# Turning the decayed keys on VectorE where they are made, in a decoder trunk on one core

## The chip, the core and the metric

The kernel runs on one core of a Trainium2 chip. A core has TensorE (PE: matmuls; a matmul first loads a stationary operand, "PEld", then streams a moving one, and writes to PSUM), VectorE (DVE), ScalarE (ACT), GpSimd (POOL) and SyncE (SP), which issues nearly all DMA here. Each engine works through its own list of instructions in order; semaphores hold an instruction until what it needs is there. DMA moves data between the device's memory (DRAM in the kernel's words) and the on-chip memory SBUF. The metric is the device time of one execution in microseconds, as the median of several runs.

## The reference

One layer of a decoder trunk over 1024 tokens of width 1024, all in float32. Two branches share one input projection: gated linear attention (GLA, 4 heads, keys of 128, values of 256) and a gated short convolution. They are merged, projected, and followed by a gated embedding and a norm. What matters here is the attention, in chunks of 64 tokens:

```python
b = jnp.cumsum(gk, axis=3)
b_last = b[:, :, :, -1:, :]
q_in = q * jnp.exp(b)
k_in = k * jnp.exp(-b)
k_dec = k * jnp.exp(b_last - b)
a = jnp.where(causal, jnp.einsum('nbhid,nbhjd->nbhij', q_in, k_in), 0.0)
o_intra = jnp.einsum('nbhij,nbhjv->nbhiv', a, v)

def step(state, xs):
    q_n, k_n, v_n, d_n = xs
    o_n = jnp.einsum('bhcd,bhdv->bhcv', q_n, state)
    state = d_n[..., None] * state + jnp.einsum('bhcd,bhcv->bhdv', k_n, v_n)
    return state, o_n
```

The state's update multiplies the decayed keys `k_dec`, turned, with the values. On TensorE the contraction runs over the partitions, so the update needs `k_dec` with tokens on the partitions, while the input projection makes it with the key's 128 features on the partitions.

## The kernel before

**Matmuls.** Nearly all work on TensorE is products of 1024-wide matrices. They are cut in quadrants by Strassen's scheme in Winograd's form (seven products for eight, classes `Cell` and `Rows`), and every float32 operand is split into a high and a low part (`split`: ScalarE copies the high part, VectorE subtracts it), so that a product is three matmuls (`mm3`). A product of one quadrant is 12 matmuls of 128x128 by 512 columns. `run_groups` runs the products in a fixed order; it asks for a product's loads up to 14 products ahead (`RING` = 8 plus 6) and for its splits up to 7 ahead.

**Order of the work.** Nothing is issued as the code runs. `Flow.note` records each instruction with a modelled cost, and finds what it depends on by blocks of `GRAIN` elements along a tile's free dimension (`View.blocks`, L122 to 130). `set_dues` gives every instruction a due time and `put_in_order` simulates the five engines and writes one order for each. The large products' matmuls (`main`) keep the program's order; the attention's matmuls come in bundles (`nc.bundle`, `close_bundle`) that are put between them when their operands are ready by the simulation.

**Where the keys are made.** In the phase "qk", `k_cons` (L1343 to 1360) takes a head's k for one half of the tokens (512) from PSUM, with the 128 features on the partitions. It fills the tile `kk`: for each of NP = 4 pairs of chunks (128 tokens) 4 x 64 columns, of which the first 128 are the scores' keys and the last 128 the decayed keys as the state needs them. One store puts both in `qkd[h][i]`, columns 384 to 640 of a row of 5 x 128 per pair. `q_cons` puts the scaled q into the first three blocks. There are 4 heads and 2 halves, so this happens 8 times.

**Where they are used.** `attend` (L1445 to 1563) goes over 8 pairs of chunks for 2 heads, twice (32 steps in all). `fetch` loads a step's 5 x 128 columns (`qkl`) and the values (`vl`) three steps ahead. `step_a` computes the scores (the float32 matmul is recorded as two instructions) and turns the decayed keys with a TensorE transpose into columns 128 to 256 of the PSUM tile `X`, except in a head's last pair, whose state nobody reads. `read_a` takes the scores through the mask and splits them (`aTh`, `aTl`), and splits the turned keys from PSUM into `keh` and `kel`. In the next bundle `step_s` multiplies these with the values for the state's update and `step_b` computes the output; `read_s` and `read_b` take them out of PSUM.

**The gate's input.** Late in the kernel `flip` turns the residual in blocks and stores it in `gd[p][j][:, i]`, from where the gate's cells load it.

`ev` (L892) is a pool of three 128x512 tiles, shared by several phases.

Of the kernel before, what the change touches and what calls it, by code (L numbers as in the profile page):

```python
# [16 lines left out]
P = 128  # L17
# [6 lines left out]
NP = HALF // P  # L24
# [18 lines left out]


PE, DVE, ACT, POOL, SP = range(5)
GRAIN = 64
TABLE = {AF.Exp: 1, AF.Ln: 2, AF.Sigmoid: 3}


class View:  # L50
# [81 lines left out]
    def place(self):  # L132
        real = self.buf.get()
        if self.dtype != self.buf.dtype:
            real = real.bitcast(self.dtype)
        a, b = self.rows
        return bass.AP(tensor=real.tensor, offset=real.offset + a * self.buf.size + self.off,
                       ap=[[self.buf.size, b - a]] + [[s, n] for s, n in self.dims])


class Buffer:
# [105 lines left out]
class Flow:  # L247
# [12 lines left out]
    def note(self, engine, op, call, args, kw):  # L260
        views = [a for a in args if isinstance(a, View) or hasattr(a, "ap")]
        views += [a for k, a in kw.items() if k not in ("out", "accum_out") and (isinstance(a, View) or hasattr(a, "ap"))]
        outs, ins = ([kw["out"]], views) if "out" in kw else (views[:1], views[1:])
        if kw.get("accum_out") is not None:
            outs.append(kw["accum_out"])
        o = Op()
        o.n, o.engine, o.call, o.args, o.kw = len(self.ops), engine, call, args, kw
        o.side, o.table, o.bytes, o.bufs, o.hurry = self.side, 0, 0, [], self.hurry
        label = lambda v: v.buf.name if isinstance(v, View) else "in"
        o.name = f"{label(outs[0])}<-{','.join(label(v) for v in ins)}"  # L270
        shape = outs[0].shape
        n = 1
        for d in shape[1:]:
            n *= d
        o.lat = 0.15
        if op == "dma_start":
            o.cost, o.bytes = 0.4, shape[0] * n * 4
            o.lat = 2.0 + o.bytes / 250e3
        elif engine == PE:
            o.cost, o.lat = n / 2400 + 0.0134, 0.22  # L280
            if op == "transpose" or args[1].dtype == F32:
                o.cost = 0.11 if op == "transpose" else 0.22
            elif args[1].shape[0] < P:
                o.cost = 0.42
        elif engine == DVE:
            psum = any(isinstance(v, View) and v.buf.pool.name == "ps" for v in outs + ins)
            o.cost = 0.07 + n * (0.00055 if op in ("tensor_scalar", "tensor_copy") and not psum else 0.00104)
            if op in ("scalar_tensor_tensor", "tensor_scalar"):
                o.cost += 0.06
            if op == "tensor_tensor_scan":  # L290
                o.cost = 0.05 + n * 0.0021
        elif engine == ACT:
            o.cost = 0.10 + n * 0.000833 + (0.1 if "accum_out" in kw else 0.0) + (0.08 if len(ins) > 1 else 0.0)
            o.table = TABLE.get(args[2] if len(args) > 2 else None, 0)
        elif engine == POOL:
            o.cost = 0.1 + n * 0.001 if op == "memset" else 0.35 + 0.25 * n
        preds = {}

        def behind(p):
            if p is not None and p != o.n:  # L300
                q = self.ops[p]
                lat = q.lat
                if q.engine == engine and not q.bytes:
                    lat = 0.0 if engine == PE else 0.08
                preds[p] = max(preds.get(p, 0.0), lat)

        for v in ins:
            if isinstance(v, View):
                for b in v.blocks():
                    e = v.buf.memory.setdefault(b, [None, []])  # L310
                    behind(e[0])
                    e[1].append(o.n)
        for v in outs:
            if isinstance(v, View):
                for b in v.blocks():
                    e = v.buf.memory.setdefault(b, [None, []])
                    for p in [e[0]] + e[1]:
                        behind(p)
                    e[0], e[1] = o.n, []
                if engine == PE:  # L320
                    behind(v.buf.group)
                    v.buf.group = o.n
                for pool in v.buf.pool.instead:
                    for old in pool.buffers:
                        for p in old.users:
                            behind(p)
        for v in outs + ins:
            if isinstance(v, View) and v.buf not in o.bufs:
                if v.buf.index is None:
                    v.buf.index = len(v.buf.tag.buffers)  # L330
                    v.buf.tag.buffers.append(v.buf)
                o.bufs.append(v.buf)
                v.buf.users.append(o.n)
        o.preds, o.succs = preds, []
        for p in preds:
            self.ops[p].succs.append(o.n)
        self.ops.append(o)
        if engine == PE and not o.side:
            self.main.append(o)
        if self.bundle is not None and engine == PE:  # L340
            self.bundle.append(o)
# [195 lines left out]
def kernel(  # L537
# [56 lines left out]
    def dram(name, *shape):  # L594
        return dr.tile([P, *shape], F32, name=name)
# [11 lines left out]
    mcd = [[dram(f"mcd{k}_{i}", HALF) for i in range(2)] for k in range(8)]  # L607
    md = [dram(f"md{i}", 2, 2, 2, 4, P) for i in range(2)]
    x2d = [dram(f"x2d{b}", D) for b in range(8)]
    gd = [[dram(f"gd{p}_{q}", 2, 4, P) for q in range(2)] for p in range(4)]  # L610
    wtd = [[dram(f"wtd{w}_{n}", 4, 512) for n in range(4 + 3 * w)] for w in range(2)]

    load = nc.sync.dma_start
# [693 lines left out]
    with phase("qk", [ph["za"]]) as qp:  # L1307
# [35 lines left out]
        def k_cons(hp):  # L1343

            def cons(i, j, src):
                h = 2 * hp + j
                nm = f"{h}_{i}"
                c4 = get_c(h, i, "k")
                kk = qp.tile([P, NP, 4, CH], F32, tag="kk", name=f"kk{nm}", bufs=2)
                dc = dcs[:, h, i]  # L1350
                tt(kk[:, :, 0:4:3, :], c4, c4[:, :, :, CH - 1:CH].to_broadcast([P, NP, 2, CH]), op=ALU.subtract)
                ex(kk[:, :, 0:4:3, :], kk[:, :, 0:4:3, :], 1.0)
                ex(kk[:, :, 1, :], c4[:, :, 1, :], 1.0)
                k4 = src.rearrange("p (n c t) -> p n c t", c=2, t=CH)
                tt(kk[:, :, 0, :], k4[:, :, 0, :], kk[:, :, 0, :], op=ALU.mult)
                tt(kk[:, :, 1:4:2, :], k4[:, :, 1:2, :].to_broadcast([P, NP, 2, CH]), kk[:, :, 1:4:2, :],
                   op=ALU.mult)
                tt(kk[:, :, 2, :], kk[:, :, 0, :], dc[:, :, 1:2].to_broadcast([P, NP, CH]), op=ALU.mult)
                store(qkd[h][i][:, :, 3 * P:5 * P], kk.rearrange("p n s t -> p n (s t)"))
            return cons  # L1360

        for hp in range(2):
# [82 lines left out]
    def attend(hp, ap, every):  # L1445
# [21 lines left out]
        def step_a(it, X):  # L1467
            pr, h = its[it]
            qk = f(ins[it][0])
            mm(X[:, 0:P], qk[:, 3 * P:4 * P], qk[:, 2 * P:3 * P], start=True, stop=True)  # L1470
            if pr < 2 * NP - 1:
                transpose(X[:, P:2 * P], qk[:, 4 * P:5 * P])

        def read_a(it, X):
            pr, h = its[it]
            nm = f"{h}_{pr}"
            a = aTf[it % 2]
            nc.vector.copy_predicated(a, trim, X[:, 0:P])
            ke = None
            if pr < 2 * NP - 1:  # L1480
                ke = (ap.tile([P, P], F32R, tag="keh", name=f"keh{nm}", bufs=2),
                      ap.tile([P, P], F32R, tag="kel", name=f"kel{nm}", bufs=2))
                split(*ke, X[:, P:2 * P])
            aT = (ap.tile([P, P], F32R, tag="aTh", name=f"aTh{nm}", bufs=2),
                  ap.tile([P, P], F32R, tag="aTl", name=f"aTl{nm}", bufs=2))
            split(*aT, a)
            scores[it] = aT, ke
# [178 lines left out]
    with phase("late", [ph["sw"], ep]) as lp:  # L1666
        flipped, rgate, both = set(), {}, [None, None]

        def make_out(p, cell):
# [18 lines left out]
            def flip(i, j):  # L1688
                pt = pso.tile([P, 4, P], F32, tag="o", name=f"pt_g{p}_{i}_{j}", bufs=2)
                for k in range(4):  # L1690
                    transpose(pt[:, k, :], xt[i][j][:, k * P:(k + 1) * P])
                g = lp.tile([P, 4, P], F32, tag="gr", name=f"gr{p}_{i}_{j}", bufs=3)
                nc.scalar.copy(g, pt)
                store(gd[p][j][:, i], g)
                yield 1
                flipped.add((p, i, j))

# [21 lines left out]

        for p in range(4):  # L1720
            make_out(p, outs[p])
        gts = [Cell(f"gt{p}", "A", [gd[p][n // 2][:, n % 2] for n in range(4)], gres, None) for p in range(4)]
        for p, c in enumerate(gts):
            c.ready = lambda k, p=p: {(p, i, j) for i in range(2) for j in range(2)} <= flipped
        with phase("sw4", lp.instead, lp) as pool:
# [183 lines left out]
```

## Time and profile before

| What | Value |
|---|---|
| median of 3 runs | 1095.49 us (1095.38 to 1095.55) |
| the profiled execution | 1095.63 us |
| its span, first to last instruction | 1093.8 us |
| mean granted TensorE clock | 0.999 |
| DMA | 241.18 MB in 157,599 packets, 220 GB/s over the span |
| stage "qk", keys made | stores of `kk` issued from 266.6 to 316.6 us |
| attention | loads of `qkl` issued from 617.7 to 727.9 us |

All engines' instructions come from helpers, so most rows name one line (L520) and are told apart by their tiles: `X<-ident,qkl` is the instruction that writes tile X and reads tiles ident and qkl. A row of a tile's view gives engine, operation, count, the shortest, median and longest duration in ns, when the first and the last began, and the shape. A row of the timeline gives the start and the length in us, then engine, operation, tiles, shape and how many instructions were merged. Matmuls overlap each other in the records, and their ends are modelled. A row of the waits names who waited, for whom, the total in us, how often, and the longest. A row by stage gives the stretch in us, its length, the busy time (and count) of PE, PEld, DVE, ACT and POOL, the granted clock, the DMA's busy share and GB/s.

### The profile page before, as it was taken

The page shows a single profiled execution, that of the slowest core. Times are in us where ns is not written, and L with a number is a line of the kernel's source. Part 1 is how long each engine was busy: PE and PEld are TensorE (multiplying, and loading weights), DVE is VectorE, ACT ScalarE, POOL GpSimd, SP SyncE. Part 2 cuts the span into 40 slices and gives each one's busy share as a digit, 9 for nine tenths or more (in the row PEclk, how much of TensorE's full clock was granted, in tenths as well). Part 3 has the DMA queues.
Part 4 walks back from the last instruction along what each step waited for, and adds up shares of the span by engine and source line. Part 5 has one row for each costly group of instructions (what it writes and reads, how often), then busy time and mean ns, then how long its engine had stood idle before and what let it go on. Part 6 is the DMA issues. An engine that isn't in the chain of part 4 may idle for free.

```text
span 1093.8 us, 15337 instructions
## 1 busy us (share of the span) xinstructions
PE 1086.0 (99%) x5042; PEld 905.4 (83%) x5042; DVE 853.7 (78%) x1391; ACT 600.4 (55%) x1115; POOL 56.8 (5%) x117
## 2 busy tenths in 40 slices
PE   9999999999999999999999999999999999999997
PEld 7888888888888888888888888888888888888886
DVE  6996477879878869748649687776999889959586
ACT  5864447876543454343334376766735445468554
POOL 0000000000000000000000022220000000001021
PEclk9999999999999999999999999999999999999999
DMA  9986463358876595212212699988594888889762
GB/s 338 338 270 208 163 201 114 108 182 256 248 235 237 191 298 190 97 53 68 87 59 76 218 312 325 344 261 283 191 340 162 308 265 286 298 303 321 262 221 101
DMA packets 157599, 241.18 MB, mean 220 GB/s; under 512 B 13520, under 2 KB 68432, under 8 KB 157520
## 3 DMA queue, kind: packets, MB, share of 16 engines
q1 hardware_dynamic: 157088, 239.75, 65.7%
q8 instruction: 39, 0.64, 0.2%
q10 hardware_dynamic: 432, 0.46, 0.1%
q14 instruction: 40, 0.33, 0.1%
HBM read 159.55 MB, written 80.61 MB: 220 GB/s over the span
## 4 chain that ended last, share of the span: by engine, by line
PE 99%; ACT 0%; DVE 0%; issue 0%; POOL 0%; POOLq 0%; ACTq 0%
PE vacc L520 7%; PE op L520 3%; PE pe L520 2%; PE X L520 2%; PE gc1Y L520 1%; PE ga3Y L520 1%; PE ga2Y L520 1%; PE gc0Y L520 1%; PE ga1Y L520 1%; PE ga0Y L520 1%; PE out1Y L520 1%; PE out3Y L520 1%; PE out0Y L520 1%; PE out2Y L520 1%; PE za2Y L520 1%; PE za0Y L520 1%
## 5 line engine op out<-in xcount | busy, mean ns | idle before, releaser
L520 ACT ACT_TABLE_LOAD x18 | 23.1, 1283 | 1.9 <-PEq L1898 1.6
L520 ACT ACTIVATE junk<-x 128x512 bf16<-128x512 f32 (+1 forms) x29 | 17.8, 613 | 8.2 <-DVE x L520 8.0
L520 DVE TENSOR_TENSOR wt<-wt 128x512 f32<-128x512 f32 x32 | 21.7, 686 | 0.6 <-DMA wtd<-wt 0.4
L520 POOL TENSOR_TENSOR or<-or,mhalf 128x1 f32<-128x1 f32 x32 | 20.5, 642 | 2.7
L520 DVE SCALAR_TENSOR_TENSOR u<-t,vec,u 128x1024 f32<-128x1024 f32 x16 | 20.4, 1277 | 0.0
L520 POOL MEMSET t<- 128x2 f32 x8 | 0.8, 100 | 377.6 <-DVE u L520 194.8
L520 ACT ACTIVATE og<-op,or 128x256 f32<-128x256 f32 x32 | 15.1, 471 | 7.7 <-POOL or L520 7.6
L520 DVE COPY_PREDICATED aT<-trim,X 128x128 f32<-128x128 int32 x32 | 9.6, 300 | 11.2 <-PE X L520 11.1
L520 POOL TENSOR_SCALAR rg<-ms 128x1 f32<-128x1 f32 x8 | 4.8, 596 | 259.7 <-ACT junk L520 259.7
L520 POOL TENSOR_SCALAR or<-oms 128x1 f32<-128x1 f32 x32 | 9.7, 303 | 124.6 <-ACT junk L520 124.5
L520 PE MATMUL op<-vl,aTh 128*128 128x256 f32 x64 | 15.2, 318 | 0.0
L520 PE MATMUL op<-Sh,qkl 128*128 128x256 f32 x56 | 14.6, 283 | 0.0
L520 DVE TENSOR_TENSOR szl<-op,szl 128x256 f32<-128x256 f32 x32 | 13.5, 422 | 1.3 <-PE op L520 0.7
L520 ACT CAST aTh<-aT 128x128 fp32r<-128x128 f32 x32 | 9.5, 297 | 8.3 <-DVE aT L520 7.9
L520 ACT ACTIVATE junk<-op 128x256 bf16<-128x256 f32 x32 | 12.3, 384 | 2.3 <-DVE szl L520 1.4
L520 PE MATMUL pe<-wpehi,pThi 128*128 128x512 f32 (+1 forms) x36 | 13.0, 383 | 0.0
L520 PE MATMUL pe<-wpehi,pTlo 128*128 128x512 f32 (+1 forms) x36 | 12.9, 376 | 0.0
L520 PE MATMUL pe<-wpelo,pThi 128*128 128x512 f32 (+1 forms) x36 | 12.7, 372 | 0.0
L520 PEld LDWEIGHTS X<-vl,keh 128*128 128x128 f32 x56 | 10.5, 188 | 2.4
L520 PE MATMUL X<-qkl 128*128 128x128 f32 x64 | 12.3, 273 | 0.0
L520 PE MATMUL op<-ident,og 128*128 128x128 f32 x64 | 12.3, 272 | 0.0
L520 DVE TENSOR_TENSOR Sl<-S,Sh 128x256 fp32r<-128x256 f32 x28 | 11.7, 418 | 0.3 <-ACT Sh L520 0.2
(3251 smaller groups left out, 4157.6 us busy)
## 6 DMA issues: line engine op xcount, KB each, us to landing
wtd<-wt SPq DMA_DIRECT2D x44, 256.0 KB, 3.8
qkl<-qkd SPq DMA_DIRECT2D x32, 320.0 KB, 5.2
wt<-in_wb_dram SPq DMA_DIRECT2D x8, 1024.0 KB, 6.7
vl<-vd SPq DMA_DIRECT2D x32, 256.0 KB, 4.9
vraw<-in_wb_dram SPq DMA_DIRECT2D x28, 256.0 KB, 4.2
wgq<-wtd SPq DMA_DIRECT2D x14, 512.0 KB, 5.7
uq<-ud SPq DMA_DIRECT2D x10, 512.0 KB, 5.9
oq<-od SPq DMA_DIRECT2D x10, 512.0 KB, 6.9
```

Source lines behind the costliest of these rows:

```text
L520: o.call(*[place(a) for a in o.args], **{k: place(a) for k, a in o.kw.items()})
```

## The change

The decayed keys are turned in `k_cons`. A VectorE transpose works on square blocks of 32x32: each block is turned in its own place, and the blocks stay where they were. The four stores that follow, one for each group of 32 partitions, put the blocks in their places: `Blocks` describes a target of 32 columns in all 128 rows of `qkd`, written from 32 partitions in runs of 32 floats. The keys of the scores are stored apart. `step_a` no longer turns anything, and `read_a` splits the decayed keys from the loaded tile. The planner's grain goes from 64 to 32 elements, it counts a block store at 10 bytes an element, and the buffers `gd` are cut in two.

```diff
-GRAIN = 64
+GRAIN = 32
...
+class Blocks(View):
+    def __init__(self, plain, s):
+        (step, n), _ = plain.dims
+        off = plain.off + 32 * s
+        super().__init__(plain.buf, (0, 32), off, [(step, n), (32 * plain.buf.size, 4), (1, 32)], plain.dtype)
+        self.columns = View(plain.buf, plain.rows, off, [(step, n), (1, 32)], plain.dtype)
+
+    def blocks(self):
+        return self.columns.blocks()
...
-            o.cost, o.bytes = 0.4, shape[0] * n * 4
+            o.cost, o.bytes = 0.4, shape[0] * n * (10 if isinstance(outs[0], Blocks) else 4)
...
-    gd = [[dram(f"gd{p}_{q}", 2, 4, P) for q in range(2)] for p in range(4)]
+    gd = [[[dram(f"gd{p}_{q}_{i}", 4, P) for i in range(2)] for q in range(2)] for p in range(4)]
...
-                store(qkd[h][i][:, :, 3 * P:5 * P], kk.rearrange("p n s t -> p n (s t)"))
+                kT = ev(f"kT{nm}").rearrange("p (n t) -> p n t", n=NP)
+                kf = kk.rearrange("p n s t -> p n (s t)")
+                nc.vector.transpose(kT, kf[:, :, P:2 * P])
+                store(qkd[h][i][:, :, 3 * P:4 * P], kf[:, :, 0:P])
+                for b in range(4):
+                    store(Blocks(qkd[h][i][:, :, 4 * P:5 * P], b), kT[32 * b:32 * b + 32].rearrange("p n (b t) -> p n b t", b=4))
...
             mm(X[:, 0:P], qk[:, 3 * P:4 * P], qk[:, 2 * P:3 * P], start=True, stop=True)
-            if pr < 2 * NP - 1:
-                transpose(X[:, P:2 * P], qk[:, 4 * P:5 * P])
...
-                split(*ke, X[:, P:2 * P])
+                split(*ke, f(ins[it][0])[:, 4 * P:5 * P])
...
-                store(gd[p][j][:, i], g)
+                store(gd[p][j][i], g)
...
-        gts = [Cell(f"gt{p}", "A", [gd[p][n // 2][:, n % 2] for n in range(4)], gres, None) for p in range(4)]
+        gts = [Cell(f"gt{p}", "A", [gd[p][n // 2][n % 2] for n in range(4)], gres, None) for p in range(4)]
```

## The prediction

> **What bounds the kernel now.** I read the chain that ended last first, then the waits of TensorE, then the chain in order of time.
>
> ```profile
> span 1093.8 us, 15337 instructions
> PE 1086.0 (99%) x5042; PEld 905.4 (83%) x5042; DVE 853.7 (78%) x1391; ACT 600.4 (55%) x1115; POOL 56.8 (5%) x117
> PE 99%; ACT 0%; DVE 0%; issue 0%; POOL 0%; POOLq 0%; ACTq 0%
> PE warm L520 <- PEq L1898: 0.8, 1, 0.8
> ```
>
> The chain is TensorE for 99% of the span, and the only wait listed for TensorE in the whole span is 0.8 us at its start. But a matmul's recorded end is modelled, and records overlap, so "99% busy" could hide gaps. The starts can't. In the chain by time, twelve matmuls of 512 columns form one product:
>
> ```profile
> 231.68 2.72 PE za3Y L520 x12
> 234.40 2.72 PE q0X L520 x12
> ...
> 253.44 2.72 PE k0X L520 x12
> 256.16 2.72 PE k0V L520 x12
> ...
> 746.63 2.73 PE gc2V L520 x12
> ...
> 1080.51 2.73 PE gt3V L520 x12
> ```
>
> 231.68 + 2.72 = 234.40: the next product begins where this one ends, and a product takes 2.72 to 2.73 us (227 ns a matmul) at 234 us as at 1080 us. TensorE runs back to back at its own issue pitch. So an instruction taken from it shortens the run by that instruction's pitch, and work added elsewhere costs nothing until TensorE waits for it.
>
> **The transposes that go.** There are fewer than a first look at the attention loop suggests: the last of eight pairs of chunks of each head has none, so 4 heads x 7 = 28.
>
> ```profile
> L520 PE MATMUL X<-qkl x64: 272/274/275, 625.9 to 737.4; 128*128 128x128 f32 x64
> L520 PEld LDWEIGHTS X<-ident,qkl x28: 140/140/143, 626.0 to 730.4; 128*128 128x128 f32 x28
> L520 PE MATMUL X<-ident,qkl x28: 272/273/273, 626.1 to 730.5; 128*128 128x128 f32 x28
> ```
>
> 273 ns is the time from start to modelled end, not what the instruction holds up. For that I take one bundle with the transpose and one without (the last pair), in TensorE's timeline:
>
> ```profile
> 636.92 0.39 PE L520 MATMUL X<-qkl 128*128 128x128 f32 x2
> ...
> 640.17 0.39 PE L520 MATMUL X<-qkl 128*128 128x128 f32 x2
> 640.39 0.27 PE L520 MATMUL X<-ident,qkl 128*128 128x128 f32 x1
> 640.42 0.48 PE L520 MATMUL op<-vl,aTh 128*128 128x256 f32 x2
> 640.74 0.28 PE L520 MATMUL op<-vl,aTl 128*128 128x256 f32 x1
> ...
> 734.25 0.39 PE L520 MATMUL X<-qkl 128*128 128x128 f32 x2
> 734.39 0.48 PE L520 MATMUL op<-vl,aTh 128*128 128x256 f32 x2
> 734.71 0.29 PE L520 MATMUL op<-vl,aTl 128*128 128x256 f32 x1
> ```
>
> From the scores' first matmul to the same later matmul: 640.74 - 640.17 = 0.57 us with the transpose, 734.71 - 734.25 = 0.46 us without. The transpose costs 0.11 us; its weight load hides. 28 x 0.11 = **3.1 us saved**. Bounds: the times are rounded to 0.01 us, so 0.10 to 0.12 each, 2.8 to 3.4 us.
>
> The Trainium skill (TensorE: Matmul & The Clock Gate, Part 4: PE-mode transpose) gives about 275 ns for such a transpose in one kernel's context. The recorded 273 ns agree with it, and the sum by it would be 28 x 0.275 = 7.7 us; the pitch in the two bundles says it is a latency, not a cost.
>
> **What is added where k is made.** Per head and half (8 times): one VectorE transpose of 128x512, and the store of 512 KB becomes a store of 256 KB and four stores of 64 KB in runs of 32 floats (128 bytes).
>
> ```profile
> L520 DVE TENSOR_TENSOR kk<-kk,dcs x8: 409/413/417, 266.2 to 316.1; 128x256 f32<-128x256 f32 x8
> L520 DVE TENSOR_TENSOR kk<-ck x8: 680/684/691, 255.5 to 313.2; 128x512 f32<-128x512 f32 x8
> L520 DVE TENSOR_TENSOR_SCAN c<-smask,t x8: 1210/1218/1220, 183.2 to 236.9; 128x512 f32<-128x512 f32 x8
> L520 SPq DMA_DIRECT2D qkd<-kk x8: 513/522/590, 266.6 to 316.6; - x8
> 240.00:350.00 110.00, 110.00 (x487) 91.09 (x486) 92.00 (x173) 55.79 (x111) 0.20 (x2) 1.00 0.81 256
> 250.00:280.00 30.00, 30.00 (x134) 24.84 (x133) 29.19 (x61) 19.06 (x41) 0.00 (x0) 1.00 0.93 279
> 340.00:350.00 10.00, 10.00 (x46) 8.29 (x45) 8.71 (x14) 2.49 (x4) 0.00 (x0) 1.00 0.89 312
> q1 hardware_dynamic: 157088, 239.75, 65.7%
> ```
>
> (The rows by stage give the stretch, its length, busy time of PE, PEld, DVE, ACT and POOL, the clock, the DMA share and GB/s.)
>
> The trace has no VectorE transpose. Below, 0.41 us (a pass over half the elements); above, 1.22 us (the scan, its slowest pass over 128x512); I take 0.68 us, the ordinary pass of this shape. 8 x 0.68 = 5.5 us (3.3 to 9.8). VectorE is idle 110 - 92 = 18 us between 240 and 350 us, so it fits, but not locally: from 250 to 280 us VectorE is busy 29.2 of 30 us, four of the eight transposes fall there or just behind, and operand splits slide by about 2.7 us. They are prepared up to 7 products ahead (7 x 2.72 = 19 us), which covers it: **0 on the path**. With that cover gone it would be 5.5 us.
>
> SyncE issues 32 more stores at about 0.52 us each, 16.7 us spread over 50 us. The four block stores wait on SyncE for the VectorE transpose, and weight loads queue behind them; these run up to 14 products ahead (the ring's 8 and 6 more in `run_groups`; 14 x 2.72 = 38 us). **0**.
>
> DMA time: the last of the stages above moves 312 / 0.89 = 350 GB/s while busy, 21.9 bytes per ns and engine, in large pieces. From 240 to 350 us 256 x 110 = 28.2 MB went through in 0.81 x 110 = 89.1 us; at 350 GB/s it would be 80.5 us. The difference, 8.6 us on 16 engines, over some 25,000 pieces (by the code, 32 stores of 512 pieces, the rest in 2 KB rows) is 5.5 ns a piece. A run of 128 bytes is then 5.9 + 5.5 = 11.4 ns, an estimate. Bounds: below 5.9 ns by bytes alone; above 73 ns, the mean piece of the big queue (0.657 x 16 x 1093.8 us / 157088). I take 11.4: 2048 runs / 16 engines make 1.5 us per head and half, the 256 KB store 0.9 us, and the old store was 1.7 us; net +0.7 us, 8 times 5.7 us, in a stage whose DMA is idle 20.9 us. **0**.
>
> **What moves in the attention.** The split of the transposed block (keh, kel) reads the loaded tile instead of PSUM.
>
> ```profile
> L520 ACT CAST keh<-X x28: 255/266/268, 626.9 to 732.2; 128x128 fp32r<-128x128 f32 x28
> L520 ACT CAST aTh<-aT x32: 285/299/301, 627.6 to 738.1; 128x128 fp32r<-128x128 f32 x32
> ACT keh L520 <- PE X L520: 0.2, 1, 0.2
> qkl<-qkd SPq DMA_DIRECT2D x32, 320.0 KB, 5.2
> 617.00:740.00 123.00, 123.00 (x740) 109.07 (x739) 92.21 (x239) 83.11 (x239) 28.88 (x62) 1.00 0.95 309
> ```
>
> A cast from SBUF is 299 - 266 = 33 ns longer: 28 x 33 = 0.9 us of ScalarE, which is idle 123 - 83 = 40 us there. The loads keep size and number. The finer bookkeeping grain (64 to 32 elements) and the gate's buffers cut in two add no instruction; they change only the order the planner writes. I price that at 0 and keep its risk as a rival.
>
> **Sum.** Against the profiled execution: span 1093.8 - 3.1 = 1090.7 us. That execution took 1095.63 us, 1.8 us around its span and 0.14 us over the median; against the median, 1095.49 - 3.1 = **1092.4 us**.
>
> **Rivals.**
>
> *Gain eaten by the new order* (1095.0 us). The planner sorts all instructions anew. After the last matmul the run goes on for 7.3 us with chains on other engines, where any order change counts in full.
>
> ```profile
> 1086.53 0.28 PE L520 MATMUL pelast<-pwhi,pwlo 128*128 128x256 f32 x1
> L520 ACT ACT_TABLE_LOAD x18 | 23.1, 1283 | 1.9 <-PEq L1898 1.6
> ```
>
> Two function-table loads more in such a place are 2 x 1.28 = 2.6 us: 1092.4 + 2.6 = 1095.0. For it: today's plan has almost no gap left, so it can hardly get better by chance. Against: the dependences of the late stages don't change.
>
> *The wait moves to ScalarE* (slower, 1103 us). The keh cast waited for TensorE, 0.2 us in all; now it waits for the qkl load, and ScalarE takes its work in order: behind a late load stand the splits of the main weights and the copies out of PSUM, for which TensorE waits next. The loads land 5.2 us after issue with the DMA 95% busy. ScalarE's 40 us idle and the 19 us of prepared operands cover 28 waits of up to 59 / 28 = 2.1 us each; at 2.5 us each the excess is 70 - 59 = 11 us, 1092.4 + 11 = 1103. Against: a block is fetched three steps ahead, about 3 x (640.17 - 636.92) = 9.8 us by the bundles' spacing, twice the landing time; TensorE needs that load too, and never waited for it.
>
> *Small stores choke the DMA* (slower, 1102 us). At 73 ns a run: 9.3 + 0.9 - 1.7 = 8.5 us, 8 times 68 us; less 20.9 us idle and 38 us of loading ahead, TensorE waits about 10 us. It decides from about 64 ns a run. The Trainium skill (DMA: Bandwidth & Descriptors, Specifications) speaks for it: pieces under 512 bytes are read, modified and written. Priced as twice the estimate, 23 ns, the stage still has room; no run so far shows such pieces in number.
>
> *The transpose costs its recorded time* (1087.8 us). 28 x 0.273 = 7.6 us. Against it stands the pitch in both bundles.
>
> **How the numbers follow.** Forecast 0.70 (its own range 1091.5 to 1093.4: the pitch's 2.8 to 3.4 us, and some 0.7 us either way for a gap or the tail); gain eaten 0.16; wait on ScalarE 0.07; small stores 0.04; full 273 ns 0.03. A difference of 0.2%, 2.2 us, is about what this kernel's measurement tells from none. Faster: 0.70 + 0.03 = 0.73; same 0.16; slower 0.11. The range runs from 1091.5 to 1096.8 us, over the eaten gain and some more, and leaves out 0.14.
>
> **What would show it.** X<-ident,qkl gone and 28 fewer matmuls than 5042; the last matmul begins near 1083.4 us; still no TensorE wait but the first; eight VectorE transposes near 0.7 us; some 16,000 more pieces under 512 bytes and a higher DMA share at 250 to 320 us; no DMA as releaser of keh. Products longer than 2.73 us in the chain, a TensorE wait on keh or on a weight split, or a tail beyond 7.3 us would make the prediction wrong, and name the rival.

## The result, and the profile after

| | before | after |
|---|---|---|
| median | 1095.65 us (1095.33 to 1096.33, 19 runs) | 1093.57 us (1092.91 to 1094.84, 19 runs) |
| profiled execution | 1095.63 us, span 1093.8 us | 1094.09 us, span 1092.3 us |

The ratio is 0.9981, interval 0.9974 to 0.9988. The change gains 2.08 us where 3.1 were forecast: the gain is there, and about 1 us of it is given back elsewhere.

The page of the kernel after, the lines that answer to those of before:

```profile
span 1092.3 us, 15330 instructions
PE 1083.6 (99%) x5014; PEld 902.3 (83%) x5014; DVE 857.1 (78%) x1399; ACT 601.6 (55%) x1116; POOL 55.6 (5%) x117
DMA packets 174496, 241.19 MB, mean 221 GB/s; under 512 B 30416, under 2 KB 85328, under 8 KB 174416
PE 97%; DMA 1%; ACT 0%; issue 0%; DVE 0%; SPq 0%; POOL 0%; POOLq 0%; DVEq 0%
```

5042 - 5014 = 28 matmuls are gone, VectorE has 8 more, and 174,496 - 157,599 = 16,897 packets were added (32 stores of 512 runs are 16,384 of them). New on the chain is 1% of DMA. To see where the time went, the span is cut at four starts: of the first product after the projection of v (q0X), of the first product after the keys (cc0X), of the last matmul, and the end. The chain by time of the kernel before, then of the kernel after (start, length, what):

```profile
72.35 76.16 PE vacc L520 x336
...
310.56 2.72 PE cc0X L520 x12
```

```profile
72.52 76.16 PE vacc L534 x336
...
234.81 2.72 PE q0X L534 x12
...
294.81 6.41 DMA qkd<-qdh
...
302.91 3.06 PE k1Y L534 x12
...
311.41 2.72 PE cc0X L534 x12
```

The last matmul and the last store in the timeline of the kernel after:

```profile
1084.28 0.28 PE L534 MATMUL pelast<-pwhi,pwlo 128*128 128x256 f32 x1
...
1087.84 0.35 ACTq L534 DMA_DIRECT2D out_dram<-x  x1
```

With the rows of before (q0X at 234.40 and the last matmul at 1086.53 us stand in the prediction), each stretch is a difference of two starts:

| Stretch | before | after | difference |
|---|---|---|---|
| start of the span to vacc | 72.35 | 72.52 | +0.17 |
| vacc to q0X | 162.05 | 162.29 | +0.24 |
| q0X to cc0X (keys made) | 76.16 | 76.60 | +0.44 |
| cc0X to the last matmul (with the attention) | 775.97 | 772.87 | **-3.10** |
| last matmul to the end | 7.3 | 8.0 | +0.7 |
| sum | 1093.8 | 1092.3 | -1.5 |

So the forecast's 3.1 us is there to the hundredth, in the stretch that holds the attention. Three other stretches lost a little each; the first row is the landing of the first load, which differs between executions of any kernel (last section).

**Vacc to q0X.** The small product zp, whose operand VectorE makes, now stands right behind that operand. The timeline of before, then of after, around it:

```profile
198.55 0.70 DVE L520 TENSOR_TENSOR low<-lowp,low 32x512 fp32r<-32x512 f32 x1
...
199.40 0.70 PE L520 MATMUL zp<-low,g 128*128 128x512 f32 x2
```

```profile
196.30 1.28 ACT L534 ACT_TABLE_LOAD   x1
...
198.07 0.70 DVE L534 TENSOR_TENSOR low<-lowp,low 32x512 fp32r<-32x512 f32 x1
...
198.46 0.39 PE L534 MATMUL za2V<-h1hi,za2lo 128*128 128x512 f32 x1
198.89 0.30 PEld L534 LDWEIGHTS zp<-low,g 128*128 128x128 f32 x2 [0.46 <-ACT za3hi L534]
198.92 0.71 PE L534 MATMUL zp<-low,g 128*128 128x512 f32 x2
```

After, the matmul ahead of zp starts at 198.46 and zp only at 198.92: 0.46 us where the pitch is 0.227. VectorE ends `low` at 198.77. Before, it ended it at 199.25 and zp came at 199.40, after a full-speed stream. The row of zp's weight load names ScalarE's cast `za3hi` for this wait, but zp doesn't read that tile, and the cast ended at 198.70 us, 0.07 us ahead of `low`. The waits listed for PE, which the prediction read, hold matmuls alone and show nothing here; this wait and the next one stand at TensorE's weight loads (PEld). The row of the function-table load is taken up below, with the rivals.

**Where the keys are made.** The waits between 240 and 350 us of the kernel after (who, for whom, total us, times, longest), and then its timeline:

```profile
ACT qdh L534 <- DMA qkd<-qdh: 5.4, 3, 2.4
...
PEld k1Y L534 <- ACT k1u L534: 0.5, 1, 0.5
```

```profile
301.24 0.62 ACT L534 CAST qdh<-Q 128x512 fp32r<-128x512 f32 x1 [2.40 <-DMA qkd<-qdh]
...
302.28 0.58 ACT L534 COPY k1u<-k1Y 128x512 f32<-128x512 f32 x1
...
302.91 0.50 PE L534 MATMUL k1Y<-h4hi,k1hi 128*128 128x512 f32 x1
```

Before, the copy `k1u` began at 300.01 us, well ahead of the next product that fills k1Y (its first weight load is at 302.01 us), in the timeline of that kernel:

```profile
300.01 0.58 ACT L520 COPY k1u<-k1Y 128x512 f32<-128x512 f32 x1
```

A store of `qdh`, issued at 294.81 us, takes 6.41 us to land (chain above). `qdh` has one buffer, so ScalarE stands 2.40 us until it may write the next one. Behind it in ScalarE's list stands the copy that empties the PSUM tile of k1Y, and TensorE waits for that: the product starts at 302.91 us. The stage as a whole has become fuller; its row after (stretch, length, busy PE, PEld, DVE, ACT, POOL, clock, DMA share, GB/s), to set beside 0.81 before:

```profile
240.00:350.00 110.00, 109.90 (x485) 90.63 (x484) 95.77 (x180) 56.14 (x111) 0.20 (x2) 1.00 0.89 257
```

**The tail.** Order and durations of the last instructions are as before: from the last matmul to the last store's issue it is 1090.06 - 1086.53 = 3.53 us before and 1087.84 - 1084.28 = 3.56 us after. The last store of before in its timeline:

```profile
1090.06 0.35 ACTq L520 DMA_DIRECT2D out_dram<-x  x1
```

What is longer is the landing of the stores. The last store in the DMA view of the stretch behind the last matmul (tensors, queue, KB, us from issue to landing), before and after:

```profile
out_dram<-x ACTq DMA_DIRECT2D x1, 192.0 KB, 2.7
```

```profile
out_dram<-x ACTq DMA_DIRECT2D x1, 192.0 KB, 3.4
```

And the queues (packets, MB, share) in the 2 us from 4.0 to 6.0 us behind the last matmul's start, before and after:

```profile
q1 hardware_dynamic: 189, 0.39, 51.7%
q10 hardware_dynamic: 144, 0.20, 27.2%
```

```profile
q1 hardware_dynamic: 198, 0.41, 56.1%
q10 hardware_dynamic: 136, 0.19, 25.3%
q14 instruction: 1, 0.01, 1.0%
```

After, one fetch of instructions (8 KB, queue 14) falls among the last stores, and they land 0.7 us later. Why it is there is what experiments 5 and 6 ask.

The new work itself, by tiles of the kernel after:

```profile
L534 SPq DMA_DIRECT2D qkd<-kT x32: 570/624/774, 268.3 to 323.0; - x32
L534 DVE STREAM_TRANSPOSE kT<-kk x8: 674/708/715, 267.5 to 319.6; 128x512 f32<-128x512 f32 x8
```

```profile
L534 ACT CAST keh<-qkl x28: 283/298/310, 625.1 to 724.0; 128x128 fp32r<-128x128 f32 x28
```

### The profile page after: what moved, and what is told of

It reads as the page before. It is cut to its first block, busy times and chain, and to the rows that moved or that the text cites. A ratio compares the mean times of both kernels' runs of the same rounds, so it can differ in the third digit from the quotient of the medians.

```text
span 1092.3 us, 15330 instructions
## 1 busy us (share of the span) xinstructions
PE 1083.6 (99%) x5014; PEld 902.3 (83%) x5014; DVE 857.1 (78%) x1399; ACT 601.6 (55%) x1116; POOL 55.6 (5%) x117
## 2 busy tenths in 40 slices
DMA packets 174496, 241.19 MB, mean 221 GB/s; under 512 B 30416, under 2 KB 85328, under 8 KB 174416
## 4 chain that ended last, share of the span: by engine, by line
PE 97%; DMA 1%; ACT 0%; issue 0%; DVE 0%; SPq 0%; POOL 0%; POOLq 0%; DVEq 0%
PE vacc L534 7%; PE op L534 3%; PE pe L534 2%; PE X L534 2%; PE ga2Y L534 1%; PE gc1Y L534 1%; PE ga3Y L534 1%; PE gc0Y L534 1%; PE ga1Y L534 1%; PE ga0Y L534 1%; PE out1Y L534 1%; PE out3Y L534 1%; PE out0Y L534 1%; PE out2Y L534 1%; PE za2Y L534 1%; PE za0Y L534 1%
## 5 line engine op out<-in xcount | busy, mean ns | idle before, releaser
L534 ACT CAST Sh<-S 128x256 fp32r<-128x256 f32 x28 | 11.3, 403 | 1.8 <-PE op L534 0.6
```

The costliest lines, as they stand in the source:

```text
L534: o.call(*[place(a) for a in o.args], **{k: place(a) for k, a in o.kw.items()})
```

## The experiments

The same four stretches for every run, from its own chain by time, the last matmul's row in its timeline, and its span. The medians were taken beside runs of the kernel before on the same chip.

| Kernel | vacc to q0X | q0X to cc0X | cc0X to last matmul | to the end | median us (runs) | ratio to before |
|---|---|---|---|---|---|---|
| before | 162.05 | 76.16 | 775.97 | 7.3 | 1095.65 (19) | |
| after | 162.29 | 76.60 | 772.87 | 8.0 | 1093.57 (19) | 0.9981 (0.9974 to 0.9988) |
| 1 no turn | 162.03 | 76.15 | 772.87 | 7.3 | 1092.68 (7) | 0.9973 (0.9962 to 0.9984) |
| 2 strips | 162.28 | 76.16 | 772.86 | 8.0 | 1093.63 (11) | 0.9980 (0.9971 to 0.9989) |
| 3 two buffers | 162.27 | 76.16 | 772.86 | 7.3 | 1092.78 (8) | 0.9973 (0.9963 to 0.9984) |
| 4 grain 32 | 162.27 | 76.16 | 775.97 | 7.3 | 1096.18 (11) | 1.0002 (0.9994 to 1.0011) |
| 5 after, 12 fills | 162.31 | 76.24 | 772.87 | 7.3 | 1092.97 (11) | 0.9976 (0.9967 to 0.9985) |
| 6 before, 23 fills | 162.02 | 76.16 | 775.96 | 8.0 | 1096.47 (11) | 1.0008 (0.9999 to 1.0017) |
| 7 both repairs | 162.04 | 76.16 | 772.87 | 7.3 | 1092.80 (8) | 0.9973 (0.9963 to 0.9984) |
| 8 grain for stores | 162.04 | 76.16 | 772.87 | 7.4 | 1092.80 (10) | 0.9974 (0.9965 to 0.9984) |
| 9 after again | 162.29 | 76.40 | 772.86 | 8.0 | 1093.36 (1) | |
| 10 two turns | 162.02 | 76.16 | 779.22 | 7.3 | 1099.18 (6) | 1.0031 (1.0019 to 1.0044) |

### 1. The saving alone: no turning at all

The kernel before without its transposes; the split reads the loaded, unturned block. It leaves out the turning of the decayed keys, so the state it computes is another.

```diff
-            if pr < 2 * NP - 1:
-                transpose(X[:, P:2 * P], qk[:, 4 * P:5 * P])
...
-                split(*ke, X[:, P:2 * P])
+                split(*ke, f(ins[it][0])[:, 4 * P:5 * P])
```

> The kernel before, with the 28 TensorE transposes left out and the decayed keys split as loaded, unturned; nothing added where k is made, grain 64. Theory (the pitch): 28 x 0.109 us = 3.1 us go and nothing is given back, so 1095.6 - 3.1 = 1092.5 us; the last matmul begins 3.1 us earlier than in the kernel before, and every product outside the attention starts where it did. Rival (a transpose is worth less on the path, about 0.08 us, since other work fills in): 2.1 us, 1093.5 us, the same as the changed kernel.

The stretch of the attention is 772.87 us, 3.10 less than before, and every other stretch is as before. So the transposes are worth 3.10 us, and the median, 3.00 us under before, is about what the change could bring if its new work cost nothing.

### 2. The same stores in long runs

In the kernel after, each of the four stores writes its 32 partitions plainly, in runs of 128 floats; the blocks are not put in place, so the keys that the state reads are misplaced. Order and number of instructions stay.

```diff
+class Strips(Blocks):
+    def __init__(self, plain, s):
+        super().__init__(plain, s)
+        View.__init__(self, plain.buf, (32 * s, 32 * s + 32), plain.off, plain.dims, plain.dtype)
...
-                    store(Blocks(qkd[h][i][:, :, 4 * P:5 * P], b), kT[32 * b:32 * b + 32].rearrange("p n (b t) -> p n b t", b=4))
+                    store(Strips(qkd[h][i][:, :, 4 * P:5 * P], b), kT[32 * b:32 * b + 32])
```

> The changed kernel, but the four stores of the turned keys put each strip of 32 partitions where it lies, in runs of 512 bytes, instead of placing the 32x32 blocks in runs of 128 bytes; same order of instructions, same bytes, the keys end up unplaced. Theory (small pieces hold up the DMA where k is made, a store lands late, ScalarE waits for its buffer and TensorE for ScalarE): no product of k1 over 2.75 us, the gap of 0.44 us at 302 us gone, about 1093.1 us. Rival (the gap comes from the number of stores or their order): the gap stays at 0.3 to 0.5 us, about 1093.6 us.

The gap at the keys is gone (76.16 us), zp's gap and the long tail stay, and the median is that of the kernel after. The stage's row and the late ScalarE cast in the timeline:

```profile
240.00:350.00 110.00, 110.00 (x487) 91.09 (x486) 96.25 (x181) 56.32 (x111) 0.20 (x2) 1.00 0.84 259
```

```profile
300.19 0.62 ACT L534 CAST qdh<-Q 128x512 fp32r<-128x512 f32 x1 [1.35 <-DMA qkd<-qdh]
```

ScalarE still waits for the store of `qdh`, but 1.35 us instead of 2.40, and TensorE doesn't notice. The short runs raise the DMA's share from 0.84 to 0.89, 0.05 x 110 = 5.5 us per engine, and make the store late, as far as one profile each can show it. Yet they aren't what costs most: the time is the same within the interval, and the 1093.1 us that was expected without the gap did not come.

The Trainium skill (DMA: Bandwidth & Descriptors, Specifications) says that pieces under 512 bytes are read, modified and written. By the shares, from 0.81 to 0.89 of 110 us, the eight turns added 8.8 us, 1.1 us each. By the prediction's sizes the old store of 1.7 us went and a smaller one of 0.9 us came, so the block stores took 1.1 + 1.7 - 0.9 = 1.9 us for 128 runs on each engine, about 15 ns a run (an estimate, shares being rounded to 0.01). That lies between the prediction's 11.4 ns and its 23 ns for pieces priced twice, so it neither shows nor excludes such a rewriting.

### 3. Two buffers where ScalarE waits

```diff
-                hi = qp.tile([P, NP, P], F32R, tag="qdh", name=f"qdh{nm}")
-                lo = qp.tile([P, NP, P], F32R, tag="qdl", name=f"qdl{nm}")
+                hi = qp.tile([P, NP, P], F32R, tag="qdh", name=f"qdh{nm}", bufs=2)
+                lo = qp.tile([P, NP, P], F32R, tag="qdl", name=f"qdl{nm}", bufs=2)
```

> The changed kernel with two buffers instead of one for the split q (qdh, qdl). Theory (ScalarE stands at the qdh cast until the store from its only buffer has landed): that wait of 2.4 us and the gap of 0.44 us behind it go, about 1093.1 us. Rival (the gap is the DMA's own lateness, for a load that TensorE or a split needs): the gap stays, about 1093.6 us.

No wait for the store of `qdh` is left, and the stretch is 76.16 us. But the gain over the kernel after is 0.79 us by the medians, more than that gap: the tail is short again, too. A buffer of `qdh` can't act there; that was the first sign that the tail hangs on something other than its own work. zp's gap stayed (162.27).

### 4. The finer grain alone

The kernel before with `GRAIN = 32`, nothing else.

```diff
-GRAIN = 64
+GRAIN = 32
```

> The kernel before with the planner's grain at 32 instead of 64 and nothing else. Theory (the finer grain alone moved the decays' bundles between 165 and 200 us and left 0.24 us of gaps there): slower than before by 0.2 to 0.3 us, 1095.9 us, with product q0X starting at 234.6 to 234.7 instead of 234.40 us. Rival (the 0.24 us came with the later due times of the changed attention): q0X at 234.40, 1095.6 us.

By the total this is inconclusive: the interval, 0.9994 to 1.0011, holds no change. The trace decides it; its chain by time:

```profile
72.73 76.16 PE vacc L520 x336
...
235.00 2.72 PE q0X L520 x12
```

235.00 - 72.73 = 162.27, against 162.05 before: the grain alone makes the 0.22 us at zp. The other stretches are as before.

### 5 and 6. The tail: shifting the instruction fetch

VectorE's list is made longer at the very start of the kernel, by fills of a column that is written over right behind them: 12 fills in the kernel after, 23 in the kernel before (VectorE has 1987 records at the end of the kernel after and 1964 before, and 1987 - 1964 = 23).

```diff
-    make_identity(tc.nc, ident.place())
+    [tc.nc.vector.memset(ident[:, 0:1].place(), 0.0) for _ in range(12)]; make_identity(tc.nc, ident.place())
```

> The changed kernel with 12 one-column memsets on VectorE ahead of all its work and nothing else (the memsets write a column that is overwritten at once). Theory (VectorE's added instructions put one more 8 KB instruction fetch 4.5 us behind the last matmul, among the last output stores, which land 0.7 us later): the fetch comes some microseconds earlier, and the time from the last matmul's start to the end goes from 8.0 to 7.3 us; about 1092.9 to 1093.2 us. The gap of 0.4 us at 302 us stays, since the order there is unchanged. Rival (the late stores were chance of that execution, or come with the data's place in memory): no relation to the pads; 1093.6 us again.

> The kernel before with 23 such memsets. Theory: VectorE's count then reaches the fetch's place in the same tail; an 8 KB fetch about 4.5 us behind the last matmul and a tail of 8.0 instead of 7.3 us, 1096.3 to 1096.6 us, part of it the memsets' own time at the start. Rival: tail 7.3 us as in the kernel before.

Both came out as expected of the fetch. With 12 fills more the kernel after has the short tail, and nothing of the instruction queue among its last stores. The queues from 4.0 to 6.0 us behind its last matmul (1083.73):

```profile
q1 hardware_dynamic: 198, 0.41, 54.0%
q10 hardware_dynamic: 144, 0.20, 27.2%
```

With 23 fills the kernel before has the long tail of the kernel after, with the fetch at the same place (4.0 to 6.0 us behind its last matmul at 1086.66):

```profile
q1 hardware_dynamic: 191, 0.39, 53.4%
q10 hardware_dynamic: 137, 0.19, 25.8%
q14 instruction: 1, 0.01, 1.5%
```

The median of the kernel before rises from 1095.79 to 1096.47, about 0.7 us, though the interval of the ratio, 0.9999 to 1.0017, just holds 1; the tail in the trace (8.0 for 7.3 us) is what shows it.

### 7 and 8. A version without the loss

In 8 the grain of 32 holds only for the buffers the block stores write; in 7 that and the two buffers of experiment 3.

```diff
-        return sorted({b for s in starts for b in range(s // GRAIN, (s + step * (n - 1)) // GRAIN + 1)})
+        grain = GRAIN if self.buf.name.startswith("qkd") else 64
+        return sorted({b for s in starts for b in range(s // grain, (s + step * (n - 1)) // grain + 1)})
```

> The changed kernel with two buffers for the split q, and a grain of 32 for the k and q store's buffer alone (64 for all others). Theory: no gap at 302 us and none between 165 and 200 us, so all of 3.1 us is kept: 1095.65 - 3.1 = 1092.5 us, if no fetch falls into the tail. Rival (any new order costs some tenths somewhere): 1092.8 us or more, as with two buffers alone.

> The changed kernel with the grain of 32 for the k and q store's buffer alone, one buffer for the split q. Theory: product q0X starts where the kernel before has it but for the start's own spread (no 0.24 us lost between 165 and 200 us); the gap at 302 us stays, 0.3 to 0.5 us. 1092.9 us, or 1093.6 us with a fetch in the tail. Rival (the gap at 302 us was chance): no gap, 1092.5 us.

The chain by time of kernel 8:

```profile
72.27 76.16 PE vacc L534 x336
...
234.31 2.72 PE q0X L534 x12
...
310.47 2.72 PE cc0X L534 x12
```

234.31 - 72.27 = 162.04: zp's gap is gone. 310.47 - 234.31 = 76.16: so is the gap at the keys, with one buffer of `qdh` and a DMA share of 0.89 still. The tail is short, since VectorE's list now ends at 1979 records and no fetch falls into it. Both versions do all the work of the kernel after, take 1092.80 us and are faster than the kernel before by 0.26 to 0.27%; against the kernel after that is 0.77 us by the medians. The second buffer adds nothing to the narrower use of the grain. For 8 the expectation was half missed: it kept the gap at the keys, which went, since the order of the instructions changed there, too (ScalarE writes `qdh` at 298.65 us without a wait). For 7 it gave 1092.5 us from a start of 1095.65; the kernel before stood at 1095.79 us beside these runs, and 2.99 of the 3.1 us were kept.

### 9. The same kernel once more

The kernel after, unchanged, in one further execution, on another chip than experiments 1 to 8.

> The changed kernel once more, for a second profiled execution. The fetch's theory: a tail of 8.0 us again, with the 8 KB fetch 4.5 us behind the last matmul; if chance, 7.3 us. The gap at 302 us was 0.44 us in its first execution and 0.08 us with twelve memsets ahead, in the same order: by the late-store theory it lies between 0 and 0.5 us and goes with how long the store of the split q takes to land at 295 us (6.4 us where the gap was 0.44 us).

Its chain by time, and the late cast in its timeline:

```profile
234.17 2.72 PE q0X L534 x12
...
302.17 2.96 PE k1Y L534 x12
...
310.57 2.72 PE cc0X L534 x12
```

```profile
300.42 0.62 ACT L534 CAST qdh<-Q 128x512 fp32r<-128x512 f32 x1 [2.21 <-DMA qkd<-qdh]
```

zp's gap (162.29) and the tail (8.0) are the same, so they belong to the program. The gap at the keys is 0.24 us here, 0.44 in the first profile and 0.08 in experiment 5, which keeps this part of the order. ScalarE's waits there were 2.21, 2.40 and 1.89 us: it has some 1.8 to 2.0 us to spare, and what the store takes beyond that is lost. This part differs from execution to execution.

### 10. The turn twice

The kernel before with each transpose issued twice.

```diff
                 transpose(X[:, P:2 * P], qk[:, 4 * P:5 * P])
+                transpose(X[:, P:2 * P], qk[:, 4 * P:5 * P])
```

> The kernel before with each of the 28 TensorE transposes done twice, one behind the other. The pitch theory: 28 x 0.109 = 3.1 us more between the attention's start and end, 1095.7 + 3.1 = 1098.8 us, nothing elsewhere. By the recorded length, 28 x 0.273 = 7.6 us, 1103.3 us.

TensorE's timeline of one bundle:

```profile
643.66 0.39 PE L520 MATMUL X<-qkl 128*128 128x128 f32 x2
643.88 0.38 PE L520 MATMUL X<-ident,qkl 128*128 128x128 f32 x2
...
644.34 0.28 PE L520 MATMUL op<-vl,aTl 128*128 128x256 f32 x1
```

From the scores to the same later matmul it is 644.34 - 643.66 = 0.68 us, where one transpose made 0.57 and none 0.46. The stretch grew by 779.22 - 775.97 = 3.25 us, the median by 3.34. The recorded 273 ns would have made it 7.6. The Trainium skill (TensorE: Matmul & The Clock Gate, Part 4: PE-mode transpose) has about 275 ns for one; as the length of one instruction the trace agrees (273 ns), as its price in a stream that never stops it doesn't.

## Why the prediction was right, and where it missed

**The saving, 3.1 us: right.** The step from 273 ns to the pitch of 0.11 us carried the whole forecast; 3.10 us was measured in the change, 3.10 without any turning, 3.25 for a second turn.

**The new work, by size: near.** The VectorE transpose took 708 ns (680 taken), the issue of a block store 624 ns (520), so 32 x 0.624 = 20.0 us of SyncE for 16.7, the cast from SBUF 298 ns (299). No DMA became the releaser of keh. All of that is hidden, as said.

**The failed step is the pricing of order: "they change only the order the planner writes. I price that at 0 and keep its risk as a rival."** The grain costs 0.24 us at zp, shown by experiments 4 and 8. That the planner moved this because of the tile `glw`, whose slices of 32 share blocks of 64 elements but not of 32, is read from the code and wasn't tried.

**The tail was left out of the sum.** The forecast kept the 7.3 us as they were, since "the dependences of the late stages don't change". They don't; but VectorE's longer list puts an instruction fetch between the last stores, +0.7 us. No step of the prediction had a term for it. Experiments 5 and 6 show it both ways.

**The "0" for DMA time holds on the mean and not at one place.** "In a stage whose DMA is idle 20.9 us" is true, and 12.1 us are idle still (0.11 x 110). But one store landed late enough, ScalarE works in order, and TensorE waited 0.08 to 0.44 us. It is a mixture of two rivals, small stores and ScalarE's order, at another tile than the prediction named (`qdh`, not keh) and at a fraction of either's price. As far as one profile each can, experiment 2 ties it to the short runs, 3 to the single buffer, 8 to the order of instructions (ScalarE writes `qdh` there at 298.65 us without a wait).

**The rivals.** "Gain eaten by the new order" was part of the truth: eaten was about 1 us, not 2.6. One table load more did come with the new order, in the groups by line of the kernel after. It isn't in the tail: it stands at 196.30 us, with ScalarE busy on both sides of it, in the very stretch that loses the 0.24 us at zp. The six kernels with that gap (after, 2, 3, 4, 5 and 9) have 19 table loads, the six without it 18. Whether the load makes `low` late, or both only come with the same order, wasn't tried.

```profile
L534 ACT ACT_TABLE_LOAD x19 | 24.4, 1283 | 2.0 <-PEq L1915 1.6
```

The wait on keh didn't come: no DMA released that cast. Small stores that choke the DMA would have needed 64 ns a run; it was about 15. The recorded length of the transpose fell with experiments 1 and 10.

**The sum as measured.** -3.10 + 0.24 + 0.7 = -2.16 us, and 0.08 to 0.44 us for the gap at the keys make -2.1 to -1.7; the medians differ by 2.08. The median lies 0.2 us beyond the likeliest case's own range (1091.5 to 1093.4), which allowed some 0.7 us for a gap or the tail where both came, and inside the whole range. Of the signs named beforehand, the fewer matmuls, the eight VectorE transposes, the short pieces and keh without a DMA releaser appeared; the last matmul at 1084.28 instead of 1083.4 us, a weight load of TensorE waiting on a copy, and a tail beyond 7.3 us were the signs against it, and they name the three losses. With the gaps taken away the forecast holds: experiment 8 gained 2.99 us by its medians.

## What to carry to other kernels

Price an instruction in a saturated stream by what it delays, from two neighbouring sequences with and without it, not by its recorded length. When a schedule has no gaps left, an edit that only changes bookkeeping is worth a test of its own: limit it to the tensors that need it, as experiment 8 does. And cut the span at fixed starts before explaining a total: here 3.10 us of gain and 1 us of loss stood in different stretches, none of which a difference of totals could have named.

## What the runs showed of the hardware

**Code comes by DMA, too, and a fetch can hit the tail.** Counting VectorE's records up to each 8 KB packet of the instruction queue in the kernel after, the packets that fit VectorE come at counts 1597, 1727, 1857 and 1984: one every 128 or so. In the kernels whose list reaches that far, the last of them comes at count 1982 to 1984. (Every kernel has another such packet between 0.7 us ahead of the last matmul's start and 2.4 us behind it, in the kernel before at 0.15 us; the counts don't put it to VectorE's list, and it goes with no change of the tail.)

| Kernel | VectorE's records at the end | fetch at that count, us behind the last matmul's start | to the end |
|---|---|---|---|
| before; 4; 10 | 1964; 1969; 1965 | none | 7.3 |
| 1; 8; 7 | 1971; 1979; 1982 | none | 7.3; 7.4; 7.3 |
| after; 2; 9; 6 | 1987 | 4.5 | 8.0 |
| 3 | 1991 | 1.7 | 7.3 |
| 5 | 1999 | 0.1 | 7.3 |

Of these, only the fetch that falls among the last stores goes with a longer tail. That it is VectorE's own list follows from these counts and from the fills of 5 and 6, which lengthen no other engine's list. How one packet of 8 KB, which took 0.31 us in the kernel after (0.47 us in experiment 6), delays the stores by 0.7 us was not tried.

**The start of the stream differs by execution.** TensorE's first long chain starts when a first weight load lands. Its row in the chain by time of experiments 1 and 2, the extremes among the runs that show it:

```profile
2.57 4.40 DMA wperaw<-in_wpo_dram
```

```profile
2.57 5.24 DMA wperaw<-in_wpo_dram
```

The load landed 0.84 us later, and vacc started 0.82 us later (72.85 for 72.03 us). So a part of the spread between runs is set in the first 8 us, and stretches that begin behind that point can be compared to a few hundredths of a us where totals can't.
